# A row-sum kernel: one load of 128 partitions issued as loads of 112, 12 and 4

## The chip, the core and the metric

The kernel runs on one core of a Trainium2 chip. The core has engines that work side by side and meet at semaphores: DVE (VectorE) and ACT (ScalarE) compute here, SP (SyncE) issues all transfers, POOL (GpSimd) only sets some constants at the start, and TensorE isn't used. Sixteen DMA engines carry the data between HBM and SBUF, the on-chip memory with 128 partitions. The metric is the device time of one execution in microseconds (us); lower is better.

## What is computed

The input is 32 x 512 rows of 1024 float32 numbers; each row is summed and multiplied by 0.5.

```
batch, seq, dim = 32, 512, 1024
x: float32 [batch, seq, dim],  multiplier: 0.5

return (np.sum(x, axis=-1) * multiplier).astype(np.float32)
```

That is 67.1 MB to read and 65.5 kB to write.

## The kernel before

**Tiling.** The 16384 rows are 128 for each of the 128 partitions. A first load, `head`, brings one row for each partition (the rows 0 to 127 of the input). Then come seven blocks, the first with 15 rows a partition and the others with 16, and then a last block of 16 rows a partition. In a block, a partition holds neighbouring rows, so each partition's part of a load is one contiguous run. Three buffers of 16 rows (`xb0` to `xb2`) take turns.

**The sums.** For the seven blocks, DVE sums all rows of the block in one reduction (L136) and multiplies by 0.5 (L142); of the seventh block (block 6) it takes eight rows, and ACT sums the other eight, one an instruction (L91, `act_row`), each with a short instruction that reads the accumulator.

**The last block** is loaded in five pieces, so that little is left to do after the last byte. In the order in which SP issues them:

- p0: rows 0 to 9 (40960 bytes a partition)
- p1: rows 10 to 13 (16384 bytes)
- p2: row 14 and the first 384 columns of row 15 (5632 bytes); this is the load that is changed
- e0: columns 384 to 735 of row 15 (1408 bytes), into a tile `end`
- e1: columns 736 to 1023 of row 15 (1152 bytes), into `end` beside two partial sums

ACT sums the rows 1, 4, 7, 9, 13 and 14 of this block. DVE sums the others with `dve_sum` (L101), which adds the two halves of a row and accumulates. Row 15 takes DVE three such sums: the 384 columns of p2, the columns of e0, and a last one over e1 and the two partial sums before it.

**Order and waits.** All loads are issued from SP's one queue, in the order of the program, through `load` (its DMA is L82): an instruction of SP that waits holds up those behind it. p2's issue waits until DVE has done with block 5, e0's until block 6 has landed, e1's until DVE has done with block 6. Behind them SP issues the store of the first seven blocks' results (L184), a store of the head's results from four partitions (L188), and at last the store of the last block's results (L214). That last store waits for a semaphore, `summed_up`, to reach 2: one count from ACT after row 14, one from DVE after its last sum.

Each load has a semaphore of its own, which a DMA raises by 16 when its data is there. ACT and DVE wait for p0, p1 and p2 in one loop over k (L194 to L204), ACT with L196 and DVE with L202.

Of the kernel before, what the change touches and what calls it, by code (L numbers as in the profile page):

```python
# [9 lines left out]
def kernel(  # L10
# [13 lines left out]
    nc = tc.nc  # L24
# [4 lines left out]
    P = nc.NUM_PARTITIONS  # L29
# [4 lines left out]
    N, D = x_flat.shape  # L34
# [4 lines left out]
    B = 16  # L39
    n_blocks = rows // B  # L40
# [5 lines left out]
    x_last = x_flat[P * own : N, :].rearrange("(p c) d -> p c d", p=P)  # L46
# [4 lines left out]
    def sbuf(name, *shape):  # L51
        return ctx.enter_context(nc.sbuf_tensor(name, list(shape), fp32)).ap()
# [8 lines left out]
    cuts = [384, 736, D]  # L61
    at = 368
    end = sbuf("end", P, at + D - cuts[1])

    def sem(name):
        return nc.alloc_semaphore(name=name)

    dve_done = sem("dve_done")
# [7 lines left out]
        counts[engine] += 1  # L76
        return counts[engine]

    def load(name, dst, src, free=None, behind=None):

        landed = sem(name)
        i = nc.sync.dma_start(out=dst, in_=src)  # L82
        if free is not None:
            i.wait_op(dve_done, free, "sem-ge")
        if behind is not None:
            i.wait_op(behind, 16, "sem-ge")
        i.then_inc(landed, 16)
        return landed

    def act_row(t, r, dst):  # L90
        return nc.scalar.activation(  # L91
            out=t[:, r, :],
            in_=t[:, r, :],
            func=mybir.ActivationFunctionType.Copy,
            scale=mul,
            accum_out=dst,
        )

    def dve_sum(row, dst, scale):
        mid = row.shape[-1] // 2  # L100
        return nc.vector.tensor_tensor_reduce(  # L101
            out=row[:, 0:mid],
            in0=row[:, 0:mid],
            in1=row[:, mid:],
            scale=scale,
            scalar=0.0,
            op0=ADD,
            op1=ADD,
            accum_out=dst,
        )  # L110

    landed_head = load("landed_head", head[:, 0, :], x_flat[0:P, :])
    cleared = marks(nc.vector.memset(column, 0.0), "dve")  # L113
    nc.scalar.wait_ge(landed_head, 16)
# [6 lines left out]
    freed = []  # L121
    blocks = []
    for b, n in enumerate(sizes):
        c0 = 1 + sum(sizes[:b])
        t = buf[b % bufs][:, 0:n, :]
        landed = load(
            f"landed{b}",
            t,
            x_rows[:, c0 - 1 : c0 - 1 + n, :],
            freed[b - bufs] if b >= bufs else None,  # L130
        )
# [5 lines left out]
                out=sums[:, c0 : c0 + h], in_=t[:, 0:h, :], axis=mybir.AxisListType.X  # L137
# [5 lines left out]
            out=res[:, c0 : c0 + h],  # L143
            in_=sums[:, c0 : c0 + h],
# [5 lines left out]
        if h < n:  # L150
            nc.scalar.wait_ge(landed, 16)
            for r in range(h, n):
                i = act_row(t, r, res[:, c0 + r : c0 + r + 1])
# [5 lines left out]
    flat = t.rearrange("p c d -> p (c d)")  # L159
    flat_last = x_last.rearrange("p c d -> p (c d)")  # L160
    bounds = [0, 10 * D, 14 * D, 15 * D + cuts[0]]

    landed = [
        load(f"landed_p{k}", flat[:, lo:hi], flat_last[:, lo:hi], free, behind)
        for k, (lo, hi, free, behind) in enumerate(
            zip(
                bounds[:-1],
                bounds[1:],
                (None, None, freed[n_blocks - 3]),
                (None, blocks[n_blocks - 3], None),  # L170
            )
        )
    ]
    landed_end = [
        load(f"landed_e{k}", end[:, to : to + hi - lo], x_last[:, B - 1, lo:hi], free, behind)
        for k, (to, lo, hi, free, behind) in enumerate(
            (
                (0, cuts[0], cuts[1], None, blocks[n_blocks - 2]),
                (at, cuts[1], D, freed[n_blocks - 2], None),
            )  # L180
        )
    ]
# [10 lines left out]
    on_act = {1, 4, 7, 9, 13, 14}  # L193
    for k, (lo, hi) in enumerate(((0, 10), (10, 14), (14, 15))):  # L194
        on = [r for r in range(lo, hi) if r in on_act]
        nc.scalar.wait_ge(landed[k], 16)  # L196
        for r in on:
            i = act_row(t, r, res[:, c0 + r : c0 + r + 1])
        if k == len(landed) - 1:
            i.then_inc(summed_up, 1)  # L200
        on = [r for r in range(lo, hi) if r not in on_act]
        nc.vector.wait_ge(landed[k], 16)  # L202
        for r in on:
            dve_sum(t[:, r, :], res[:, c0 + r : c0 + r + 1], mul)  # L204
    dve_sum(t[:, B - 1, 0 : cuts[0]], end[:, at - 2 : at - 1], 1.0)
    nc.vector.wait_ge(landed_end[0], 16)
    second = dve_sum(end[:, 0 : cuts[1] - cuts[0]], end[:, at - 1 : at], 1.0)

    second.then_inc(landed_end[1], 1)
# [75 lines left out]
```

## Time and profile before

| what | value |
|---|---|
| time, median of 3 runs | 160.55 us (160.5 to 160.6) |
| the profiled execution's own time | 160.47 us |
| its span, first to last instruction | 159.2 us |
| DVE busy | 119.1 us, 75% of the span |
| ACT busy | 17.4 us, 11% |
| DMA packets | 2168 |
| p2: 704 KB, issue to landing | 20.8 us |
| e0: 176 KB, issue to landing | 19.2 us |
| e1: 144 KB, issue to landing | 10.8 us |
| last store: 8 KB, issue to landing | 1.4 us |

The page of a profile gives busy times of engines, the DMA queue, and the chain of work that ended last, followed back from the end. The waits say which engine waited for whom. The timeline lists instructions in order of time: start in us from the span's start, duration in us, engine, line, operation, output from input with their shapes, how many of them are merged into the line, and in brackets how long the engine was idle before it and what ended that. `SPq` is the queue of SP, where DMAs are issued. Busy time of a DMA issue is the time that SP takes to issue, not the transfer. The time around the span (160.47 - 159.2 = 1.27 us) has no instruction in it.

### The profile page before, as it was taken

To read this page: it belongs to the slowest core of one execution; us is meant where nothing else is said; L and a number is where in the kernel's file an instruction comes from. 1 tells how busy PE (TensorE), PEld (TensorE's weight loads), DVE (VectorE), ACT (ScalarE), POOL (GpSimd) and SP (SyncE) were. 2 spreads that over 40 slices of the span, in tenths; PEclk is the share of its full clock that TensorE was granted. 3 is DMA by queue.
4 is the path that set the end of the run, shared out by engine and by line. 5 is a ranking of instruction groups with operands and counts; after the bars stand their busy time and mean duration, and the time that the engine had idled before them with its cause. 6 is when DMAs were issued, how large, how long until landed. Compare 5 with 4: busy or idle time off the path is not lost.

```text
span 159.2 us, 131 instructions
## 1 busy us (share of the span) xinstructions
DVE 119.1 (75%) x40; ACT 17.4 (11%) x31; POOL 0.2 (0%) x4
## 2 busy tenths in 40 slices
DVE  0000059995799968999599995999959999598376
ACT  2300000000000000000000000000000000397384
POOL 0000000000000000000000000000000000000000
DMA  9997996996997999969969969969989799798994
GB/s 379 494 401 340 494 527 264 527 527 264 527 461 329 527 395 395 527 280 511 527 264 527 527 264 527 494 296 527 445 346 527 346 445 527 329 453 371 420 401 151
DMA packets 2168, 67.18 MB, mean 422 GB/s; under 512 B 504, under 2 KB 760, under 8 KB 1016
## 3 DMA queue, kind: packets, MB, share of 16 engines
q1 hardware_dynamic: 2168, 67.18, 98.0%
HBM read 67.11 MB, written 0.07 MB: 422 GB/s over the span
## 4 chain that ended last, share of the span: by engine, by line
DMA 74%; DVE 24%; another core or an unknown queue 1%; SPq 1%; issue 0%
DMA xb<-in_x_dram 74%; DVE sums L136 22%; DVE xb L101 1%; SPq L82 1%; DVE end L101 0%; DVE res L142 0%; DVE res L101 0%
## 5 line engine op out<-in xcount | busy, mean ns | idle before, releaser
L136 DVE TENSOR_REDUCE sums<-xb 128x16 f32<-128x16384 f32 (+2 forms) x7 | 110.9, 15849 | 28.4 <-DMA xb<-in_x_dram 28.4
L91 ACT ACTIVATE xb<-xb 128x1024 f32<-128x1024 f32 x14 | 14.6, 1045 | 137.1 <-DMA xb<-in_x_dram 137.1
L101 DVE CUSTOM_DVE_ANT_0 xb<-xb 128x512 f32<-128x512 f32 (+1 forms) x10 | 5.9, 652 | 4.4 <-DMA xb<-in_x_dram 4.4
L91 ACT ACTIVATION_READ_ACCUMULATOR xb<-xb 128x1 f32 x14 | 2.6, 187 | 0.0
L113 DVE MEMSET column<- 128x32 f32 x1 | 0.1, 85 | 3.0 <-PEq L26 3.0
L117 DVE STREAM_TRANSPOSE row<-column 128x32 f32<-128x32 f32 x1 | 0.2, 212 | 2.6 <-ACT head L91 2.6
L91 ACT ACT_TABLE_LOAD x1 | 1.3, 1283 | 3.1 <-DVE column L113 3.1
L142 DVE TENSOR_SCALAR res<-sums 128x16 f32<-128x16 f32 (+2 forms) x7 | 1.2, 174 | 0.2
L91 ACT ACTIVATE head<-head 128x1024 f32<-128x1024 f32 x1 | 1.1, 1056 | 0.0
L101 DVE DVE_READ_ACCUMULATOR2_ANT res<- 128x1 f32 x10 | 0.8, 80 | 0.0
L101 DVE CUSTOM_DVE_ANT_0 end<-end 128x176 f32<-128x176 f32 (+1 forms) x2 | 0.7, 326 | 0.0
L91 ACT ACTIVATION_READ_ACCUMULATOR head<-head 128x1 f32 x1 | 0.2, 186 | 0.0
L101 DVE DVE_READ_ACCUMULATOR2_ANT end<- 128x1 f32 x2 | 0.2, 82 | 0.0
L266 POOL MEMSET const-bfloat16-1.0<- 128x1 bf16 x1 | 0.1, 101 | 0.0
L266 POOL MEMSET const-uint8-127<- 128x1 uint8 x1 | 0.1, 101 | 0.0
L266 POOL MEMSET const-float32-0.0<- 128x1 f32 x1 | 0.1, 98 | 0.2 <-issue 0.2
L266 POOL MEMSET const-float32-1.0<- 128x1 f32 x1 | 0.1, 98 | 0.0
## 6 DMA issues: line engine op xcount, KB each, us to landing
xb<-in_x_dram SPq DMA_DIRECT2D x1, 7680.0 KB, 21.2
xb<-in_x_dram SPq DMA_DIRECT2D x1, 5120.0 KB, 33.6
xb<-in_x_dram SPq DMA_DIRECT2D x1, 2048.0 KB, 36.4
xb<-in_x_dram SPq DMA_DIRECT2D x1, 704.0 KB, 20.8
head<-in_x_dram SPq DMA_DIRECT2D x1, 512.0 KB, 3.3
end<-in_x_dram SPq DMA_DIRECT2D x1, 176.0 KB, 19.2
end<-in_x_dram SPq DMA_DIRECT2D x1, 144.0 KB, 10.8
xb<-in_x_dram SPq DMA_DIRECT2D x6, 40.8
```

The source lines that it names most:

```text
L82: i = nc.sync.dma_start(out=dst, in_=src)
L91: return nc.scalar.activation(out=t[:, r, :], in_=t[:, r, :], func=mybir.ActivationFunctionType.Copy, scale=mul, accum_out=dst,)
L101: return nc.vector.tensor_tensor_reduce(out=row[:, 0:mid], in0=row[:, 0:mid], in1=row[:, mid:], scale=scale, scalar=0.0, op0=ADD, op1=ADD, ...
L113: cleared = marks(nc.vector.memset(column, 0.0), "dve")
L117: turned = nc.vector.transpose(out=row, in_=column)
L136: nc.vector.reduce_sum(out=sums[:, c0 : c0 + h], in_=t[:, 0:h, :], axis=mybir.AxisListType.X),
L142: scaled = nc.vector.tensor_single_scalar(out=res[:, c0 : c0 + h], in_=sums[:, c0 : c0 + h], scalar=mul, op=mybir.AluOpType.mult,)
L266: nc = _bacc.Bacc("TRN2", target_bir_lowering=False, num_devices=1)
```

## The change

`load` gets an argument `groups`, a list of numbers of partitions. It issues one DMA for each group, one after the other over the partitions, all counting the same semaphore by 16; a wait that the load has stands on the first of them. p2 gets the groups 112, 12 and 4, all others get one group of 128. The waits for p0, p1 and p2 on ACT and DVE are for 16 times the number of groups, so those for p2 are for 48. The wait for e0 is written in the same way and stays at 16.

```diff
-    def load(name, dst, src, free=None, behind=None):
+    def load(name, dst, src, free=None, behind=None, groups=(P,)):
 
         landed = sem(name)
-        i = nc.sync.dma_start(out=dst, in_=src)
-        if free is not None:
-            i.wait_op(dve_done, free, "sem-ge")
-        if behind is not None:
-            i.wait_op(behind, 16, "sem-ge")
-        i.then_inc(landed, 16)
+        p0 = 0
+        for n in groups:
+            i = nc.sync.dma_start(out=dst[p0 : p0 + n], in_=src[p0 : p0 + n])
+            if free is not None and p0 == 0:
+                i.wait_op(dve_done, free, "sem-ge")
+            if behind is not None and p0 == 0:
+                i.wait_op(behind, 16, "sem-ge")
+            i.then_inc(landed, 16)
+            p0 += n
+        assert p0 == P
         return landed
...
+    groups = ((P,), (P,), (112, 12, 4))
     landed = [
-        load(f"landed_p{k}", flat[:, lo:hi], flat_last[:, lo:hi], free, behind)
-        for k, (lo, hi, free, behind) in enumerate(
+        load(f"landed_p{k}", flat[:, lo:hi], flat_last[:, lo:hi], free, behind, parts)
+        for k, (lo, hi, free, behind, parts) in enumerate(
             zip(
                 bounds[:-1],
                 bounds[1:],
                 (None, None, freed[n_blocks - 3]),
                 (None, blocks[n_blocks - 3], None),
+                groups,
             )
         )
     ]
...
-        nc.scalar.wait_ge(landed[k], 16)
+        nc.scalar.wait_ge(landed[k], 16 * len(groups[k]))
...
-        nc.vector.wait_ge(landed[k], 16)
+        nc.vector.wait_ge(landed[k], 16 * len(groups[k]))
...
-    nc.vector.wait_ge(landed_end[0], 16)
+    nc.vector.wait_ge(landed_end[0], 16 * len(groups_end))
```

More of the change, by code (lines that the diff above doesn't have):

```diff
@@ L173 @@
     ]
+    groups_end = (P,)
     landed_end = [
-        load(f"landed_e{k}", end[:, to : to + hi - lo], x_last[:, B - 1, lo:hi], free, behind)
-        for k, (to, lo, hi, free, behind) in enumerate(
-            (
-                (0, cuts[0], cuts[1], None, blocks[n_blocks - 2]),
-                (at, cuts[1], D, freed[n_blocks - 2], None),
+        load(
+            f"landed_e{k}",
+            end[:, to : to + hi - lo],
+            x_last[:, B - 1, lo:hi],
+            free,
+            behind,
+            parts,
+        )
+        for k, (to, lo, hi, free, behind, parts) in enumerate(
+            (
+                (0, cuts[0], cuts[1], None, blocks[n_blocks - 2], groups_end),
+                (at, cuts[1], D, freed[n_blocks - 2], None, (P,)),
             )
```

## The prediction

> **What bounds the kernel now.** I read the page's chain and DMA queue first, then the waits of all engines, then the chain and the engines' timelines over the last 10 us, then SP's, and last the semaphore updates that the trace keeps for every load.
>
> ```profile
> q1 hardware_dynamic: 2168, 67.18, 98.0%
> HBM read 67.11 MB, written 0.07 MB: 422 GB/s over the span
> ...
> DMA 74%; DVE 24%; another core or an unknown queue 1%; SPq 1%; issue 0%
> ```
>
> The 16 DMA engines are busy 98% of the span and the chain is mostly their transfers. The change adds and removes no byte, so what counts is who does the last bytes and what follows them. The chain's end:
>
> ```profile
> 118.39 36.35 DMA xb<-in_x_dram
> 154.75 0.02 issue
> 154.77 0.69 DVE xb L101
> ...
> 156.69 0.27 DVE xb L101
> 156.97 0.37 DVE end L101 x3
> 157.34 0.02 issue
> 157.36 0.31 DVE end L101
> ```
>
> From 154.77 on, DVE works without a pause: rows 10, 11 and 12 of the piece before ours (p1), then the 384 columns of our load (p2) at 156.69, then the two short loads (e0, e1). The store waits for DVE and ACT together, and ACT's timeline shows how level they are:
>
> ```profile
> 154.77 1.06 ACT L91 ACTIVATE xb<-xb 128x1024 f32<-128x1024 f32 x1 [0.62 <-DMA xb<-in_x_dram]
> 155.73 0.19 ACT L91 ACTIVATION_READ_ACCUMULATOR xb<-xb 128x1 f32 x1
> 156.50 1.06 ACT L91 ACTIVATE xb<-xb 128x1024 f32<-128x1024 f32 x1 [0.58 <-DMA xb<-in_x_dram]
> 157.47 0.19 ACT L91 ACTIVATION_READ_ACCUMULATOR xb<-xb 128x1 f32 x1
> ```
>
> ACT starts row 14 at 156.50, when p2 has landed, and ends at 157.66; DVE ends at 157.67; SP issues the store at 157.70. So **p2's landing sets ACT's end, p1's landing sets DVE's**. The reader should take an asymmetry from this. If p2, e0 and e1 land earlier, DVE still ends at 157.67, because p1 lies ahead of p2 and is untouched: the gain is at most some 0.02 us. If p2 lands later, ACT passes on all of it but about 0.01 us.
>
> **What is taken out and put in: issuing.** One issue becomes three on SP's queue.
>
> ```profile
> 135.65 0.33 SPq L82 DMA_DIRECT2D xb<-in_x_dram  x1
> 137.75 9.05 SPq L82 DMA_DIRECT2D end<-in_x_dram  x2
> 146.91 0.37 SPq L184 DMA_DIRECT2D out_dram<-res  x1
> 147.33 0.64 SPq L188 DMA_DIRECT2D out_dram<-row  x1
> ```
>
> An issue costs 0.33 us for a full load and 0.64 us for the store of four partitions, the only narrow one. Two more cost 2 x 0.33 to 2 x 0.64, 0.66 to 1.28 us with pauses of 0.05 us: SP is done by 136.7 to 137.4 instead of 135.98. Queued behind is e0's issue, which stands until block 6 lands (137.73) anyway. The cover is at least 0.3 us, so the cost is 0. Without that cover e0 would be issued a little later, and it is issued 18 us before the engines come to it, so still 0. The waits on DVE and ACT count to 48 instead of 16, the same instruction: 0.
>
> **What moves: the shares of the engines.** A load of 128 partitions runs on 16 engines: the trace has 16 updates of its semaphore. The store of four partitions has one update at its issue and four at its landing: I read four engines with one row each. Between these two rows I take 112 partitions as 16 engines with 7 rows, 12 as 12 engines with one, 4 as four with one. Then four engines carry 9 rows of p2, eight carry 8, four carry 7. One row costs (156.50 - 154.77) / 8 = 0.216 us, from p1's landing to p2's.
>
> The 16 updates of p2 come between 156.04 and 156.48 us, in two sets: eight up to 156.15, eight from 156.21. Each load shows the same two sets. From the packets at the very end, the four-row store runs on engines of the early set. Those have a lead of 0.33 to 0.44 us before the last, so one more row (0.216) and two more semaphore packets (9 ns each) fit: 0. Engines with 7 rows end 0.216 earlier; if the last is among them, p2 lands up to 0.2 us earlier, worth 0.02 us by the asymmetry. Counted in rows alone the change gives -0.02 to 0, the low end of its cost.
>
> **The unknown: do neighbouring rows get in each other's way?** In every load so far all 16 engines write 128 partitions at once. Now 12 engines write 12 neighbouring partitions, and then 4 write 4 neighbours. Each engine's 0.216 us a row may be the engine's own limit (extra cost 0) or that of the place in SBUF it writes to. For that second case I choose groups of four adjacent partitions that accept one engine's rate together: four rows then take 4 x 0.216 = 0.86 us instead of 0.216. The first engines would spend 7 x 0.216 = 1.51, then 0.86 in the load of 12, then 0.86 in that of 4: 3.24 us against 1.73, so 1.51 more. Less their lead of about 0.4, p2's last landing moves by **+1.1 us**, to 157.6. No row measures it; the nearest is the four-row store, whose packets of 128 B took 13 ns each, too small and spread over partitions 0, 32, 64 and 96. The steadiness of the large loads fits both cases.
>
> I take the sharing case. The engines' common pace of 5,632 B in 0.216 us (26 GB/s), held by all 16 through each load, looks more like a path with one fixed width than like 16 independent readers, and even a third of the price shows at the end, since nothing there absorbs a late p2.
>
> [...]
>
> **The sum.** Issuing 0, waits 0, shares -0.02 to 0, sharing +1.1 (0 to +1.1 by the bounds above). A p2 at 157.6 starts ACT's row 14 at 157.6; 1.16 us later the store goes. DVE has the 384 columns (0.28), e0 (0.37, landing 0.47 us after p2) and e1 (0.31, landing 0.83 us after p2) behind it: the same 1.16. The profiled execution took 160.47 us, 159.2 of span and 1.27 around it; with 1.1 it is 161.57. It stands 0.08 below the median of 160.55, so I predict **161.6 us**.
>
> **The rivals.**
> - *The load of 112 collides as well.* Seven rows an engine need not keep the engines on places of their own as eight may do. Each collision of two doubles some of its 1.51 us. Against it: nothing shows it. With a third to all of that on top, 0.5 to 1.5 us, the time is 162.1 to 163.1.
> - *Half the sharing.* Pairs instead of fours: 0.216 x (7 + 2 + 2) = 2.38 against 1.73, 0.65 less the lead of 0.4: +0.25, 160.8.
> - *Not slower: the lead swallows it.* The pace is the engine's own. Place: the early set, which has 0.33 to 0.44 us in hand; price: the ninth row, 0.216 us, and it decides as long as a row adds less than that lead to the early engines. For it: the two sets are in every load. Then p2 lands between 156.27 and 156.48 and DVE ends at 157.67 as now: 160.5.
> - *Faster by more than 0.3 us.* DVE's 2.9 us after p1 would have to shrink or p1 to land earlier; p1's rows precede p2's on every engine. I see no mechanism: 160.2 stands for it.
> - *It doesn't do what it says*: if the small loads went onto fewer engines than they have rows, at worst all 16 rows onto one, that engine would carry 7 + 16 rows instead of 8: 15 x 0.216 = 3.2 us less 0.4, 163.3. Held within the first rival's chance; the four updates of the narrow store speak against it.
>
> **How the numbers follow.** Full sharing 0.52 (161.6, own range 161.1 to 162.1), the load of 112 on top 0.13, half sharing 0.08, swallowed by the lead 0.22, faster 0.05. The range from 160.4 to 162.5 takes in the swallowed case, half and full sharing and a third of the first rival: 0.86; cutting it above 160.5 would lose 0.22. A measurement of this kernel can tell about 0.2% (0.3 us) from no change. Slower by more: 0.52 + 0.13 + half of 0.08, about 0.70. Within: 0.22 and the rest of 0.08, 0.25. Faster: 0.05.
>
> **What the next profile would show.** Packets: 16 + 12 + 4 semaphore packets for p2 instead of 16, so 2184 in all; fewer or more prove my shares wrong. SP's three issues over before 137.7. p1 landing at 154.75 still. If I am right, ACT's wait before row 14 grows from 0.58 to about 1.7 us, DVE gets a pause of about 0.9 us before the 192-wide sum, the chain's end runs through ACT's row 14 or the sums behind p2, and the store goes at 158.8. If ACT still starts row 14 by 156.5 and the store goes at 157.7, neighbours don't share and the prediction is wrong; a start between shows partial sharing. If p1's landing moves, the account of the end is wrong from its first step.

## The result: 162.07 us, and the profile after

The changed kernel takes 162.07 us (median of 5 runs, 161.99 to 162.21), the one before 160.54 us in the same session (160.5 to 160.6). The ratio is 1.0096, 95% interval 1.0085 to 1.0106: slower by 1.53 us. The forecast was 161.6 us, with a range of 160.4 to 162.5.

The page of the changed kernel, in the parts that were shown of before:

```profile
span 160.9 us, 133 instructions
...
q1 hardware_dynamic: 2184, 67.18, 97.8%
...
DMA 64%; DVE 32%; another core or an unknown queue 1%; SPq 1%; ACT 1%; issue 0%
```

The bytes are the same and the packets are 16 more, as 16 + 12 + 4 semaphore packets instead of 16 give. The DMA engines still count as busy for almost all of the span, and yet it is 1.7 us longer: busy engines, but slower ones. The last pieces of the chain (start, duration, what):

```profile
136.59 21.65 DMA xb<-in_x_dram
158.24 0.02 issue
158.26 1.15 ACT xb L95 x2
```

The chain's end has moved. Before, it ran from p1's landing through six sums on DVE; now it runs from the landing of p2 at 158.24 through ACT's row 14. ACT's timeline from p1's landing on:

```profile
154.97 1.06 ACT L95 ACTIVATE xb<-xb 128x1024 f32<-128x1024 f32 x1 [0.77 <-DMA xb<-in_x_dram]
155.93 0.19 ACT L95 ACTIVATION_READ_ACCUMULATOR xb<-xb 128x1 f32 x1
158.26 1.06 ACT L95 ACTIVATE xb<-xb 128x1024 f32<-128x1024 f32 x1 [2.15 <-DMA xb<-in_x_dram]
159.23 0.18 ACT L95 ACTIVATION_READ_ACCUMULATOR xb<-xb 128x1 f32 x1
```

Row 14 starts at 158.26 instead of 156.50, after a wait of 2.15 instead of 0.58 us. DVE has to wait for the same load, where it had no pause before. Its sum over the first columns of row 15, before and after:

```profile
156.62 0.35 DVE L101 CUSTOM_DVE_ANT_0 xb<-xb 128x192 f32<-128x192 f32 x1
...
158.26 0.36 DVE L105 CUSTOM_DVE_ANT_0 xb<-xb 128x192 f32<-128x192 f32 x1 [1.37 <-DMA xb<-in_x_dram]
```

SP's queue shows that issuing isn't the reason: the three issues of p2 together take 1.13 us and are over at 136.84, before e0's issue at 137.81, and only the last store has moved, from 157.70 to 159.44:

```profile
135.71 1.13 SPq L84 DMA_DIRECT2D xb<-in_x_dram  x3
137.81 9.07 SPq L84 DMA_DIRECT2D end<-in_x_dram  x2
...
159.44 0.34 SPq L228 DMA_DIRECT2D out_dram<-res  x1
```

Where the time went is seen best in one window for each kernel, from the start of p1's work to the start of row 14 (window, its length, busy time of DVE, ACT and POOL with the number of instructions, clock, DMA share, GB/s). Before:

```profile
154.77:156.50 1.73, 1.73 (x5) 1.15 (x2) 0.00 (x0) 1.00 1.00 387
```

And after:

```profile
154.97:158.26 3.29, 1.92 (x6) 1.15 (x2) 0.00 (x0) 1.00 0.98 228
```

The DMA engines are as busy as before (0.98 against 1.00), but they move 228 instead of 387 GB/s, and the window is 1.56 us longer. The single packets (one for each partition) say the same: p2's packets of 5632 bytes took 216 ns on average before, 215 to 224; now they take 293 ns, 215 to 644. Three quarters of them take over 275 ns, so the slowness isn't confined to the last 16 partitions.

Not all of the delay lies in the packets. Before, the last packet of p2 ended at 156.04 and the last count of its semaphore came at 156.48, 0.44 us later; now these are 157.18 and 158.24, 1.06 us apart. Of the 1.76 us by which row 14 starts later, 1.14 are there in the packets and 0.62 come between the last packet and the last count. The same gap is 0.45 us with three DMAs by columns and 0.81 to 1.23 us in all the kernels below that load p2 in groups of 112 or 64 partitions. What holds the counts back the trace doesn't name.

### The profile page after: what moved, and what is told of

Read it like the earlier page. It is cut to its first block, busy times and chain, and to the rows that moved or that the text cites. A ratio compares the mean times of both kernels' runs of the same rounds, so it can differ in the third digit from the quotient of the medians.

```text
span 160.9 us, 133 instructions
## 1 busy us (share of the span) xinstructions
DVE 119.1 (74%) x40; ACT 17.4 (11%) x31; POOL 0.2 (0%) x4
## 2 busy tenths in 40 slices
DMA packets 2184, 67.18 MB, mean 418 GB/s; under 512 B 520, under 2 KB 776, under 8 KB 1032
## 3 DMA queue, kind: packets, MB, share of 16 engines
q1 hardware_dynamic: 2184, 67.18, 97.8%
## 4 chain that ended last, share of the span: by engine, by line
DMA 64%; DVE 32%; another core or an unknown queue 1%; SPq 1%; ACT 1%; issue 0%
DMA xb<-in_x_dram 64%; DVE sums L140 32%; SPq L84 1%; ACT xb L95 1%; DVE res L146 0%
```

## Experiments

Theory S, from the prediction: engines that write neighbouring partitions at the same time share a way into SBUF, and the narrow loads do that (the later expectations call it theory W, for where the engines write, and a rival by which only the bytes count is B there). Rival S-wide: the load of 112 does it as well. Rival I: three DMAs cost by themselves. Rival R: the collisions are on the side of HBM, where the engines read. Further, the unequal shares of the engines (9 rows on four of them) could be the cost. The edits are shown against the changed kernel or, where it says so, against that with p2 in one DMA of 128 partitions, which is the kernel before. Each ratio is to the kernel before in the same session, which took 160.49 to 160.56 us.

| kernel | time, us | ratio to before (95%) | from p1's work to row 14, us | mean of p2's packets, ns |
|---|---|---|---|---|
| before | 160.54 | | 1.73 | 216 |
| after: 112, 12, 4 | 162.07 | 1.0096 (1.0085 to 1.0106) | 3.29 | 293 |
| three DMAs by columns | 160.66 | 1.0007 (0.9997 to 1.0016) | 1.89 | a third of the size: 79 |
| 112 alone | 161.25 | 1.0043 (1.0028 to 1.0058) | 2.34 | 296 |
| 112, 16 | 162.04 | 1.0096 (1.0081 to 1.0111) | 3.42 | 307 |
| 64, 64 | 162.47 | 1.0115 (1.0098 to 1.0132) | 3.26 | 389 |
| 112, 12, 4 from another place in HBM | 162.06 | 1.0091 (1.0072 to 1.0110) | 3.15 | 311 |

### Three DMAs of whole width: does their number cost?

```diff
-    groups = ((P,), (P,), (112, 12, 4))
+    groups = ((P,), (P,), (P, P, P))
...
+            i = nc.sync.dma_start(out=dst[:, lo:hi], in_=src[:, lo:hi])
```

> The load of row 14 and 384 columns is cut into three DMAs by columns (469, 469 and 470 of 1408), each of 128 partitions; the wait stays at 48. Theory S (engines that write neighbouring partitions share a way in): no engine leaves its rows, packets of a third of 5632 B take a third of 215 ns each, about 72 to 80 ns, and the time is 160.5 to 160.7 us. Rival I (three DMAs cost by themselves: two more issues, 32 more semaphore packets, seams between transfers): the same three DMAs, so about 162.0 us.

It took 160.66 us, and the ratio's interval holds 1. The timeline of ACT and DVE shows the old order: the 192-wide sum, over the first columns of row 15, starts 0.04 us after the readout of row 12's sum begins, as good as no pause:

```profile
156.16 0.69 DVE L107 CUSTOM_DVE_ANT_0 xb<-xb 128x512 f32<-128x512 f32 x1
156.78 0.08 DVE L107 DVE_READ_ACCUMULATOR2_ANT res<- 128x1 f32 x1
156.82 1.06 ACT L97 ACTIVATE xb<-xb 128x1024 f32<-128x1024 f32 x1 [0.74 <-DMA xb<-in_x_dram]
156.82 0.36 DVE L107 CUSTOM_DVE_ANT_0 xb<-xb 128x192 f32<-128x192 f32 x1
```

Three issues, 48 counts and the seams between transfers cost at most 0.3 us (the interval's upper end, 0.16% of 160.5), not 1.53. Rival I falls.

### The 112 alone

```diff
-    groups = ((P,), (P,), (112, 12, 4))
+    groups = ((P,), (P,), (112,))
```

The assertion that the groups fill all 128 partitions is left out as well.

> Only the DMA of 112 partitions is issued; the loads of 12 and 4 partitions are left out and the waits count 16 (row 14 and the first 384 columns of row 15 hold old data in 16 partitions). Theory S-small, as predicted (only the narrow loads collide): packets at 215 ns, 7 x 0.215 = 1.51 us after p1, landing earlier than before, and 160.5 us because DVE's work after p1 sets the end. Theory S-wide (the 112 collide as well, since seven rows an engine cross the places that eight keep apart): packets of about 300 ns as in the changed kernel's trace, 7 x 0.30 = 2.1 us, p2 lands 0.4 us later than before, 160.9 us or more, as e0 starts among engines out of step. Rival I (cost by number of DMAs): 160.5 us.

It took 161.25 us, slower than before although an eighth of p2 isn't loaded. ACT's and DVE's wait for p2:

```profile
157.31 1.06 ACT L94 ACTIVATE xb<-xb 128x1024 f32<-128x1024 f32 x1 [1.19 <-DMA xb<-in_x_dram]
157.31 0.36 DVE L104 CUSTOM_DVE_ANT_0 xb<-xb 128x192 f32<-128x192 f32 x1 [0.42 <-DMA xb<-in_x_dram]
```

The packets took 296 ns: 7 x 0.296 = 2.07 us against 7 x 0.216 = 1.51 without collisions. So the load of 112 is slow by itself, and the prediction's choice for it (no cost) is wrong. From p1's work to row 14 it takes 2.34 us, 0.83 more than those 1.51; in the kernel's time that is 0.69 us (0.43% of 160.56) of the 1.53. The other 0.84 come with the 12 and 4, and the time for their bytes is in that (one row is 0.216 us).

### Equal shares: 112 and 16

```diff
-    groups = ((P,), (P,), (112, 12, 4))
+    groups = ((P,), (P,), (112, 16))
```

> Groups of 112 and 16: every engine has 7 + 1 rows, so the shares of the engines are as before, and only the places differ. S-small: 1.51 + 4 x 0.216 = 2.37 us against 1.73, +0.65, 161.2 us. S-wide: 2.1 us for the 112 and 0.3 to 0.86 for the 16, +0.7 to +1.2, 161.2 to 161.7 us with packets of 300 ns among the 112. Rival I: one extra DMA of the two, half the change's cost, 161.3 us. If the engines' unequal shares (9 rows on four of them) were the cost: 160.5 us.

It took 162.04 us, as long as the change, with one DMA fewer and with the same 8 rows on every engine. So neither the unequal shares nor the third DMA matters; that where the rows go does is what is left, and the runs below test it. The time is above every expectation. The last packets fit that: the trace has five that start after 156.3 us and take 487 to 631 ns, up to three times 216.

### Two halves

```diff
-    groups = ((P,), (P,), (112, 12, 4))
+    groups = ((P,), (P,), (64, 64))
```

> Groups of 64 and 64: two DMAs, 16 engines with 4 rows in each, shares as before. [...] Rival I: one extra DMA, 161.3 us, packets at 215 ns.

It took 162.47 us. Its packets are 389 ns on average, the middle half of them 375 to 417: most near 400, not the 215 of rival I. This fits two engines that share a way all the time (2 x 215 = 430) better than four (4 x 215 = 860). The prediction's groups of four, an assumption, fit less: they would give 215 where each engine has four neighbouring rows, and so a group to itself, and up to 860 where the rows are dealt out one by one. The trace names neither engines nor places, so which partitions share a way is not shown. The window from p1's work to row 14 has 216 GB/s:

```profile
155.47:158.73 3.26, 1.93 (x7) 1.15 (x3) 0.00 (x0) 1.00 0.91 216
```

The window opens at 155.47, 0.7 us later than before (0.1 of it is there already in p0's rows). I read this as engines that are done with p1, start on the first half and hold up those that still write p1. In its packets this shows only once: one of p1's took 866 ns, the others up to 625, against 621 before.

### The same places in SBUF, another place in HBM

```diff
+    flat_near = x_flat[0 : 2 * P, :].rearrange("(p c) d -> p (c d)", c=2)[:, 0 : D + cuts[0]]
...
-        load(f"landed_p{k}", flat[:, lo:hi], flat_last[:, lo:hi], free, behind, parts)
+        load(f"landed_p{k}", flat[:, lo:hi], flat_near if k == 2 else flat_last[:, lo:hi], free, behind, parts)
```

> The changed kernel, with the groups 112, 12 and 4, but p2 reads its 5632 bytes for each partition from another place in HBM: the first 256 rows of the input, 8 KB apart from partition to partition instead of 64 KB (so row 14 and the first 384 columns of row 15 are sums of other data). Theory W (the collisions are where the engines write, in SBUF): the destinations are the same, so packets of 5632 B keep a mean of about 293 ns and the time is 162.0 us. Rival R (the collisions are where they read: partitions 64 KB apart in HBM fall on the same places once the engines leave their usual eight rows): another pitch, packets back to about 216 ns, 160.5 to 160.8 us.

162.06 us with packets of 311 ns. With partitions 8 KB instead of 64 KB apart in HBM nothing gets better. That speaks against rival R; the next pair reads the same rows and changes only where they are written.

### Four narrow loads, to neighbours and spread

Against the kernel before, four extra loads of the same 16 rows, between p2 and e0:

```diff
+    spare = sbuf("spare", P, D + 384)
...
+    for j in range(4):
+        i = nc.sync.dma_start(
+            out=spare[16 * j : 16 * j + 16, :], in_=flat_last[112:P, bounds[2] : bounds[3]]
+        )
+        i.then_inc(extra, 16)
...
+    nc.sync.wait_ge(extra, 64)
```

In the second kernel only the destination differs, `out=spare[j : j + 106 : 7, :]`: the partitions 0, 7, 14 to 105, then 1, 8, 15 to 106, and so on.

> The kernel before, with p2 in one DMA, and behind it four loads more of 16 rows each (the rows of partitions 112 to 127 of p2, four times) into a spare tile at neighbouring partitions: 0 to 15, 16 to 31, 32 to 47, 48 to 63. Each engine gets one row of each load, four rows more in all. Theory W (four neighbouring partitions take data at one engine's rate together): 4 x 4 x 0.216 = 3.46 us before e0, 164.0 us, less where engines run on to the next load and so spread; packets of up to 860 ns. Rival R or B (the place in SBUF doesn't matter): 4 x 0.216 = 0.86 us more, 161.4 us, packets of 216 ns.

> [...] Theory W: packets of 216 ns with some pairs at up to 430, 0.86 to 1.7 us before e0, 161.4 to 162.2 us, and clearly less than with neighbours. Rival R or B: the same time as with neighbours, 161.4 us. If narrow loads as such were slow, whatever their partitions: as slow as with neighbours, 164 us.

Neighbours: 163.35 us, ratio 1.0170 (1.0152 to 1.0189), +2.86 us over the 160.49 of their session. Spread: 161.77 us, ratio 1.0074 (1.0058 to 1.0089), +1.28 us. The two kernels differ in the partitions of the destination alone, and 1.58 us lie between them. The sum over e0's columns, which are queued behind the extra loads, waits in the first:

```profile
159.59 0.34 DVE L106 CUSTOM_DVE_ANT_0 end<-end 128x176 f32<-128x176 f32 x1 [2.08 <-DMA end<-in_x_dram]
```

and in the second:

```profile
158.28 0.34 DVE L106 CUSTOM_DVE_ANT_0 end<-end 128x176 f32<-128x176 f32 x1 [1.27 <-DMA end<-in_x_dram]
```

The last 30 packets took 505 to 551 ns with neighbours, 215 to 339 ns when spread. That is a cost of the place that is written in SBUF, since the rows read are the same. It is less than the 3.46 us that four engines on each way in lockstep would give; as I read it, engines that get ahead go on to the next load, whose 16 partitions lie elsewhere. The spread loads aren't free of collisions either, by their packets of up to 339 ns: 1.28 us against 4 x 0.216 = 0.86 for the bytes.

### The two narrow loads behind a whole p2

Against the kernel before, the 12 and 4 partitions once more into the spare tile:

```diff
+    for lo, hi in ((112, 124), (124, P)):
+        i = nc.sync.dma_start(
+            out=spare[lo:hi, :], in_=flat_last[lo:hi, bounds[2] : bounds[3]]
+        )
+        i.then_inc(extra, 16)
```

> The kernel before, with p2 in one DMA of 128 partitions, and behind it two loads more, of 12 and of 4 partitions (112 to 123 and 124 to 127, the same rows of p2 a second time), into a spare tile; nothing computes on them. Theory S (narrow loads collide by themselves): the first four engines spend 0.86 + 0.86 us in them, less a lead of 0.4 us: e0 and e1 land up to 1.3 us later, 161.8 us. Rival B (bytes alone: one row more on twelve engines and two on four): 0.2 us later at most, 160.7 us.

161.82 us, ratio 1.0077 (1.0061 to 1.0093): as theory S had it, but not by the way it had in mind. ACT's wait for p2:

```profile
157.66 1.06 ACT L96 ACTIVATE xb<-xb 128x1024 f32<-128x1024 f32 x1 [1.69 <-DMA xb<-in_x_dram]
```

p2 itself lands 1.16 us later than before (157.66 against 156.50), though the narrow loads are queued behind it. Engines that are through with their share of p2 go on to the narrow loads and write to partitions 112 to 127 while other engines still have their p2 rows for those places to write: this is how I read it; which engines these are the trace doesn't name. It is not shown, and the packets of p2 don't show the delay: of the 144 packets of this size, only the last three took over 233 ns (414 to 674). They all had ended by 156.73, and p2's last count came at 157.64, 0.91 us later. The pair above has the same effect, and there the place decides: ACT starts row 14 at 157.14 behind neighbours and at 156.60 when they are spread, against 156.50 before.

### A large block in halves: the lasting rate

With p2 in one DMA, block 3 (64 KB a partition) in two loads:

```diff
+            groups=(64, 64) if b == 3 else (P,),
...
-        nc.vector.wait_ge(landed, 16)
+        nc.vector.wait_ge(landed, 32 if b == 3 else 16)
```

> The kernel before, with p2 in one DMA, but block 3, a large load of 64 KB for each partition, goes out as 64 and 64 partitions (its waits count 32). [...] If the loss in the small halves came from seams and starts and not from a lasting limit, packets return to 2.42 us after the first and the time is 161 to 162 us.

182.06 us, ratio 1.1338 (1.1305 to 1.1371) to the 160.63 of its session. The windows, the first with block 1, the next two with block 3:

```profile
21.60:40.90 19.30, 16.32 (x2) 0.00 (x0) 0.00 (x0) 1.00 1.00 435
...
60.00:80.00 20.00, 17.39 (x2) 0.00 (x0) 0.00 (x0) 1.00 0.94 193
80.00:100.00 20.00, 0.00 (x0) 0.00 (x0) 0.00 (x0) 1.00 0.92 200
```

For 40 us the engines are busy (0.94 and 0.92) at less than half of the rate, and DVE waits:

```profile
101.38 17.22 DVE L141 TENSOR_REDUCE sums<-xb 128x16 f32<-128x16384 f32 x1 [23.23 <-DMA xb<-in_x_dram]
```

The block's packets of 65536 bytes took 5.12 instead of 2.42 us (median), from its beginning to its end. If two engines share a way there, they move 2 x 65536 bytes in 5.12 us, 25.6 GB/s, hardly less than one engine alone (65536 / 2.42 = 27.1 GB/s). So the loss lasts; if they share, the 216 ns for a row (5632 / 216 = 26.1 GB/s) fit a limit of the way that one engine already fills.

## Why the prediction was right, and where it was not

- **What bounds the end, and the asymmetry: right.** p2's landing sets ACT's end, and the delay came through nearly in full: row 14 starts 1.76 us later and the store goes 1.74 us later (159.44 against 157.70). The profiled execution took 162.21 us, 1.74 more than the 160.47 of before. By the medians it is 1.53: the profiled one is the longest of the five runs.
- **p1's landing untouched: not quite.** ACT starts on p1 at 154.97 instead of 154.77. Of the 0.20 us, 0.05 are there already at p0 (149.93 against 149.88). The rest is no chance of one execution: counted from p0's last semaphore count, p1's comes 5.03 to 5.08 us later in all four kernels with a load of 112, 5.48 with the halves, and 4.87 to 4.90 in the kernel before and the five others. By the prediction's own words its account of the end then fails at the first step, though by 0.15 us only: what is queued behind p1 does touch it. That engines which enter p2 early get in the way of those still in p1 would fit, but isn't shown.
- **Issuing and waits at 0: right.** 1.13 us for three issues, within the 0.66 to 1.28 of two more on top of 0.33, over before 137.7; the three DMAs by columns put the whole of it at 0.1 us, not to be told from none.
- **Shares at 0: right.** 2184 packets confirm 16, 12 and 4 engines, and 112 with 16 is as slow with equal shares.
- **Sharing, the forecast's term of +1.1 us: that neighbours get in each other's way was right (1.58 us between the neighbouring and the spread loads), the size and the division weren't.** No run shows the groups of four at one engine's rate that the term is worked out from; in its place the runs showed a load of 112 that is slow by itself and narrow loads that cost less than put down. p2's landing moved by 1.76 us, of which 1.1 had been put down, all of it to the narrow loads on four engines, and the load of 112 to nothing. The load of 112 alone cost 0.69 us; with 12 and 4 it is 1.53, so 0.84 come with the narrow loads. The step that failed is the "7 x 0.216 = 1.51" for the load of 112, no collision with seven rows an engine. That it collides as well was the first rival, with a chance of 0.13 and 0.5 to 1.5 us on top of the 1.1; the slowing happened at 0.69 us, and the narrow loads cost less than put down, so the time lies in the forecast's own range and just short of this rival's 162.1. That it lies within 0.5 us of the 161.6 is in part luck: a term left out and a term put too high (1.1 against 0.84) offset each other. The packets of the halves fit such groups poorly: 389 ns, where they would give 215 or up to 860, by how the rows are dealt out. The prediction's queue of 7, 4 and 4 rows on the same four engines, less a lead of 0.4 us, isn't the path: with equal shares the time is the same.
- **The lead of the early engines** was to absorb a row. It did not protect: with equal shares, where no engine has a row more, the time is the same, and loads queued behind p2 delayed p2 itself. That the engines that are ahead run on to places where others still write is my reading. Nor are the two sets of counts in each load, as the prediction has it: in the first two blocks the ninth count follows the eighth by 0.01 and 0.06 us, within the spacing of the others.
- **Half the sharing, swallowed by the lead, faster:** none of them happened. Half the sharing gave 160.8, the lead 160.5, and both lie outside 161.99 to 162.21.

Left open: how the rows of a load of 112 are dealt to the engines, which of them meet, and which partitions share a way. The packets of the halves (389 ns on average) fit two engines that meet, but the trace has no address. Open is also what delays the counts after the last packet. No version that beats the kernel before came out of these runs; moving rows from late to early engines without leaving their ways wasn't tried, since no grouping of partitions in one DMA was found that does it.

## What to carry to other kernels

Cut a load by columns when it has to be in pieces, not by partitions: three DMAs of 128 partitions cost 0.1 us here, not to be told from none, three that divide the partitions 1.5 us, and 64 + 64 more than doubled the large block's transfer. A DMA share near 1 isn't full speed (here 0.98 with 228 GB/s, 1.00 with 387 before): read it with the GB/s and with the mean time of packets of one size (293 and 216 ns). Before evening out work between DMA engines, look at what the last load gates: here an earlier landing could gain 0.02 us, and a later one cost all of it.

## What the runs showed that I had not expected

- Sharing seems to cost more than it divides: 5.12 us for two packets of 65536 bytes, if they are on one way, where 2 x 2.42 = 4.84 would do: 6% on top.
- A load that is queued behind another on the same queue can delay the one ahead: 12 and 4 partitions behind p2 moved p2's own landing by 1.16 us, and the halves of p2 moved p1's by some 0.6 us.
- The small loads behind p2 suffer too: e0's packets of 1408 bytes went from 60 to 142 ns on average in the changed kernel, but e1's landing came no further behind p2's for it (0.55 us against 0.83 before): all of e0's packets had ended by 157.95, before p2's last count at 158.24.
